# Second MLP product by Strassen's scheme on one core, with the second norm ahead of the MLP

## The chip, the cores and the metric

The kernel runs on one core of a Trainium2 chip. Its time is the device time of one execution in microseconds. A profiled execution has a time of its own and a span, from its first instruction to its last. The engines are called TensorE (PE in the rows; PEld is its weight load), VectorE (DVE), ScalarE (ACT), GpSimd (POOL) and SyncE (SP, here only a queue that issues DMAs).

## What is computed

One layer of a decoder over 512 tokens of width 1024, in float32. The attention part ends in the residual `x`; what matters here follows it:

```python
merged = gates[:, :, 0] * (y_a @ w_branch_a[l]) + gates[:, :, 1] * (y_b @ w_branch_b[l])
x = x + merged @ w_out[l]
h2 = rmsnorm(x, mlp_norm_g[l])
x = x + jnp.square(jax.nn.relu(h2 @ w_ff1[l])) @ w_ff2[l]
return rmsnorm(x, final_norm_g)
```

The hidden width is 4096: `w_ff1` is 1024 x 4096, `w_ff2` 4096 x 1024.

## The kernel before

All large products keep float32 accuracy with three matmuls in a rounded format (F32R): an operand is split into a rounded part `hi` and the rest `lo`, and `mm3` (lines 141 to 146) sums hi·hi, hi·lo and lo·hi in one PSUM buffer. Weights come by DMA as 128 x 1024 blocks into four raw buffers (`wr_p`, tag wraw); `pre` (lines 106 to 125) casts the block to `hi` on ScalarE (line 122) and subtracts to get `lo` on VectorE (line 124). `use` asks for a block and for the next two of a fixed list.

TensorE runs in the order of the code. For the other engines and the DMA queue a planner orders the instructions ahead of time, by when it expects them to be ready, the earlier in the code first; each engine then works through its list in order and waits where an operand or a buffer is not ready. PSUM has four buffers of 128 x 512 for the products (`pl_tile`).

The output projection (`out_proj`, lines 852 to 865) does, for each of four blocks of 128 tokens, two column halves of 24 matmuls; VectorE adds them to the residual `acc`, and the sum times the gain of the second norm goes to `xg` (line 863; GpSimd, for block 3 VectorE). `h2_block` (lines 867 to 875) transposes `xg` on TensorE, behind the first half of the next block, splits the result into `h2h` and `h2l`, and takes the sum of squares. The factor of the norm itself is not applied there: relu and square let its square, `r2`, be multiplied in behind the second product (line 918).

The MLP (lines 882 to 984) has 8 groups of 4 hidden blocks of 128. The first product of a hidden block is 24 matmuls of 512 tokens (`ff1_mm`); blocks 0 and 1 are done in halves of 256 tokens around `h2_block(3)` (lines 951 to 956). `ff1` takes relu (ScalarE), the square both on GpSimd and rounded on ScalarE, and their difference on VectorE. The second product of a group (`ff2`) is, for each of 4 token blocks and 2 column halves, 12 matmuls into one PSUM buffer and one VectorE instruction that scales and adds to `acc`. Between groups TensorE goes from the second product of one to the first product of the next; the last group's first product is done ahead of the second product before it, so the last two second products follow one another directly. In the last group `final` (lines 923 to 947) makes the final norm: squares on ScalarE, product with the gain and the root on GpSimd, scaling on ScalarE and VectorE, and the stores.

Of the kernel before, what the change touches and what calls it, by code (L numbers as in the profile page):

```python
# [21 lines left out]
NB = S // 128  # L22
# [27 lines left out]
def body(nc, tc, ctx, a, out, dbg=lambda name, ap: None):  # L50
# [10 lines left out]
    def sbpool(st, name, bufs=1, side="left"):  # L61
        return st.enter_context(tc.tile_pool(name=name, bufs=bufs, side=side, reuse_waits="tile"))
# [8 lines left out]
    def utile(i, dt, name):  # L71
        return u_p.tile([128, 4, S], dt, tag=f"u{i}", name=name)
# [11 lines left out]
    def pl_tile():  # L84
        return psL.tile([128, S], F32, tag="pl", name="pl")
# [15 lines left out]
        src["out", i] = a["wout"][i * 128:(i + 1) * 128]  # L101
    for i in range(32):
        src["ff1", i] = a["wff1"][i]
        src["ff2", i] = a["wff2"][i * 128:(i + 1) * 128]

    def pre(key):
        if key in W:
            return
        wh = pools.get(key[0], wh_p)
        if key[0] == "ff2":  # L110
            wh = wh2 if key[1] % 8 < 4 else ff["w"]
# [12 lines left out]
        eng.tensor_tensor(lo, raw, hi.bitcast(F32), op=ALU.subtract)  # L124
        W[key] = (hi, lo)
# [678 lines left out]
    pools["ff2"] = wh2  # L804
    mgh = m_p.tile([128, NK, S], F32R, name="mgh")
    mgl = m_p.tile([128, NK, S], F32R, name="mgl")
    gt = {}
# [68 lines left out]

    for b in range(NB):
        out_proj(b, b - 1 if b else None)
    dbg("x2", acc)


    FG = 4
    ff_st = ExitStack()
    ff = {}
    Z = {}

    def ff1_mm(p, f, lo=0, hi=S):
        wh_, wl_ = W["ff1", f]
        mm3(p[:, lo:hi], [(wh_[:, k], wl_[:, k], h2h[k][:, lo:hi], h2l[k][:, lo:hi]) for k in range(NK)])

    def ff1(f, p=None):
        use(("ff1", f), 2 if f < 30 else 31 - f)
        g, j = divmod(f, FG)
        if j == 0:
            Z[g] = (utile(2 * (g % 2), F32R, "zh"), utile(2 * (g % 2) + 1, F32R, "zl"))
        zh, zl = Z[g]
        if p is None:
            p = pl_tile()
            ff1_mm(p, f)
        r = ff["p"].tile([128, S], F32, tag="r", name="r", bufs=2)  # L900
        act.activation(r, p, AF.Relu)  # L901
        sq = ff["p"].tile([128, S], F32, tag="sq", name="sq", bufs=2)
        pool.tensor_tensor(sq, r, r, op=ALU.mult)  # L903
        act.activation(zh[:, j], r, AF.Square)
        dve.tensor_tensor(zl[:, j], sq, zh[:, j].bitcast(F32), op=ALU.subtract)  # L905

    def ff2(g):
        zh, zl = Z[g]
        w2 = [W["ff2", FG * g + j] for j in range(FG)]
        last = g == 32 // FG - 1  # L910
        for b in range(NB):
            sl = slice(b * 128, (b + 1) * 128)
            cuts = (0, 512, 768, 1024) if last and b == NB - 1 else (0, 512, 1024)
            for e, (lo, hi) in enumerate(zip(cuts, cuts[1:])):
                cs = slice(lo, hi)
                p = pl_tile()[:, :hi - lo]
                mm3(p, [(zh[:, j, sl], zl[:, j, sl], w2[j][0][:, cs], w2[j][1][:, cs]) for j in range(FG)])
                dve.scalar_tensor_tensor(acc[:, b, cs], p, r2[:, b:b + 1], acc[:, b, cs], op0=ALU.mult,  # L918
                                         op1=ALU.add)
                if last:  # L920
                    final(b, e, cs)
# [27 lines left out]
    ng = 32 // FG  # L949
    use(("ff1", 0))  # L950
    p01 = [pl_tile() for _ in range(2)]
    ff1_mm(p01[0], 0, 0, 256)
# [5 lines left out]
    ff["p"] = sbpool(ff_st, "ff", 2, "right")  # L958
    ff["w"] = sbpool(ff_st, "wh3", 4, "right")
    for j in range(FG):  # L960
        ff1(j, p01[j] if j < 2 else None)
        if j == 0:
            rsqrt_mean(r2, ss2, D)
            pool.tensor_tensor(r2, r2, r2, op=ALU.mult)
            xf = ff["p"].tile([128, 1, 512], F32, name="xf", bufs=1)
            fo = {}
            ss3 = cst.tile([128, 3 * NB], F32, name="ss3")
            r3 = cst.tile([128, NB], F32, name="r3")
        pre(("ff2", j))
    for g in range(ng):  # L970
        if g == 2:
            gf = ff["p"].tile([128, D], F32, name="gf", bufs=1)
            sp.dma_start(gf, bc(a["gfin"], [128, D]))
            pool.tensor_scalar(gf, gf, float(D) ** 0.5, None, op0=ALU.mult)
        early = FG if g == ng - 2 else 1
        if g + 1 < ng:
            for j in range(early):
                ff1(FG * (g + 1) + j)
            for j in range(FG):
                pre(("ff2", FG * (g + 1) + j))  # L980
# [51 lines left out]
```

## Time and profile before

| | |
|---|---|
| runs, median (lowest to highest) | 719.27 us (718.83 to 719.3) of 3 |
| profiled execution, time | 719.13 us |
| its span | 717.4 us |
| mean granted TensorE clock | 0.998 |
| busy: TensorE, VectorE, ScalarE, GpSimd | 705.0, 431.9, 305.8, 210.0 us |
| output projection ends, MLP begins | 360.87 us |

A row of a timeline gives the start in the span, the duration, engine, line, operation, what is written from what, the shape and the number of instructions merged; in brackets the idle time of the engine ahead of it and what ended that. Matmuls overlap: the distance of two starts is what one costs in a dense stretch.

### The profile page before, as it was taken

Reading aid. Unit: us, or ns where it says so; the run is one execution under the profiler, and the core shown is the slowest. Engines: PE = TensorE matmul, PEld = TensorE weight load, DVE = VectorE, ACT = ScalarE, POOL = GpSimd, SP = SyncE. Lnnn points to the kernel's source line nnn. Section 1 sums busy time; section 2 is a strip of 40 time slices with the busy share of each in tenths; the row PEclk is TensorE's granted clock in tenths of the full one; section 3 lists DMA queues with packets and bytes.
Section 4 is the critical chain, followed back from the end, with each engine's and each line's share of the span. In section 5 each row is a group of like instructions: output and inputs, shape, how many; then the busy total and the mean of one; then the engine's idle time right before and its main releaser. Section 6 shows DMA issues by size and latency. Waiting matters only on the chain.

```text
span 717.4 us, 10009 instructions
## 1 busy us (share of the span) xinstructions
PE 705.0 (98%) x3731; PEld 571.2 (80%) x3732; DVE 431.9 (60%) x804; ACT 305.8 (43%) x546; POOL 210.0 (29%) x236
## 2 busy tenths in 40 slices
PE   9999999999999999999999999999999999999996
PEld 7879787768765777888898888888888888888885
DVE  6487899999998855682357353353534535335233
ACT  6566777654643536651355051330513315035013
POOL 2315487663165531322132021020201203012012
PEclk9999999999999999999999999999999999999999
DMA  8632522113301128870056052241502415021002
GB/s 315 226 111 89 154 89 74 45 48 99 116 33 46 46 89 313 288 265 28 1 176 227 8 176 59 87 148 30 176 29 89 147 29 176 30 64 56 0 20 97
DMA packets 25953, 77.16 MB, mean 108 GB/s; under 512 B 3569, under 2 KB 4465, under 8 KB 25905
## 3 DMA queue, kind: packets, MB, share of 16 engines
q1 hardware_dynamic: 25040, 75.45, 31.5%
q10 hardware_dynamic: 864, 1.08, 0.4%
q8 instruction: 29, 0.48, 0.3%
q14 instruction: 20, 0.16, 0.1%
HBM read 69.31 MB, written 6.29 MB: 105 GB/s over the span
## 4 chain that ended last, share of the span: by engine, by line
PE 83%; DVE 12%; issue 1%; DMA 1%; POOL 1%; ACT 1%; SPq 0%; POOLq 0%; DVEq 0%; ACTq 0%
PE pl L144 19%; PE pl L145 19%; PE pl L146 19%; PE pl L240 3%; PE pl L241 3%; PE pl L242 3%; DVE nmx L593 2%; DVE oh L717 2%; PE pl L850 2%; PE pl L848 2%; PE pl L849 2%; DVE sc L404 2%; DVE m L403 2%; PE po L761 1%; PE pa L240 1%
## 5 line engine op out<-in xcount | busy, mean ns | idle before, releaser
L122 ACT ACTIVATE whi<-wraw 128x1024 fp32r<-128x1024 f32 (+1 forms) x103 | 108.0, 1053 | 217.4 <-PE pl L146 88.7
L124 DVE TENSOR_TENSOR wlo<-wraw,whi 128x1024 fp32r<-128x1024 f32 (+1 forms) x92 | 118.7, 1298 | 81.3 <-ACT whi L122 80.8
L903 POOL TENSOR_TENSOR sq<-r 128x512 f32<-128x512 f32 x32 | 49.2, 1540 | 245.7 <-ACT r L901 245.7
L144 PE MATMUL pl<-h2h,whi 128*128 128x512 f32 (+1 forms) x272 | 102.5, 377 | 0.0
L145 PE MATMUL pl<-h2l,whi 128*128 128x512 f32 (+1 forms) x272 | 102.4, 377 | 0.0
L146 PE MATMUL pl<-h2h,wlo 128*128 128x512 f32 (+1 forms) x272 | 102.4, 377 | 0.0
L146 PE MATMUL pl<-whi,zl 128*128 128x512 f32 (+1 forms) x260 | 100.3, 386 | 0.0
L145 PE MATMUL pl<-wlo,zh 128*128 128x512 f32 (+1 forms) x260 | 100.3, 386 | 0.0
L144 PE MATMUL pl<-whi,zh 128*128 128x512 f32 (+1 forms) x260 | 100.3, 386 | 0.0
L918 DVE SCALAR_TENSOR_TENSOR acc<-pl,r,acc 128x512 f32<-128x512 f32 (+1 forms) x65 | 48.2, 741 | 86.2 <-PE pl L146 86.2
L146 PEld LDWEIGHTS pl<-h2h,wlo 128*128 128x128 f32 x272 | 51.2, 188 | 9.4
L144 PEld LDWEIGHTS pl<-h2h,whi 128*128 128x128 f32 x272 | 51.2, 188 | 9.4
L145 PEld LDWEIGHTS pl<-h2l,whi 128*128 128x128 f32 x272 | 51.2, 188 | 9.3
L144 PEld LDWEIGHTS pl<-whi,zh 128*128 128x128 f32 x260 | 48.8, 188 | 9.9
L146 PEld LDWEIGHTS pl<-whi,zl 128*128 128x128 f32 x260 | 48.8, 188 | 9.9
L145 PEld LDWEIGHTS pl<-wlo,zh 128*128 128x128 f32 x260 | 48.8, 188 | 9.8
L717 DVE TENSOR_SCALAR oh<-posbc,thr 128x400 bf16<-128x400 f32 (+31 forms) x128 | 46.0, 411 | 3.9 <-PE pl L738 3.9
L598 POOL TENSOR_SCALAR pra<-pra,rs 128x400 f32<-128x400 f32 (+31 forms) x32 | 34.4, 1082 | 35.4 <-DVE rs L597 35.3
L240 PE MATMUL pl<-hh,whi 128*128 128x512 f32 x112 | 44.7, 399 | 0.0
L242 PE MATMUL pl<-hh,wlo 128*128 128x512 f32 x112 | 43.7, 390 | 0.0
L241 PE MATMUL pl<-hl,whi 128*128 128x512 f32 x112 | 43.7, 390 | 0.0
L905 DVE TENSOR_TENSOR zl<-sq,zh 128x512 fp32r<-128x512 f32 x32 | 22.8, 713 | 29.6 <-POOL sq L903 29.6
(287 smaller groups left out, 1305.7 us busy)
## 6 DMA issues: line engine op xcount, KB each, us to landing
wraw<-wff SPq DMA_DIRECT2D x64, 512.0 KB, 3.6
wraw<-wF SPq DMA_DIRECT2D x24, 512.0 KB, 3.3
gd<-gt SPq DMA_DIRECT2D x16, 256.0 KB, 2.2
wraw<-wbr SPq DMA_DIRECT2D x8, 512.0 KB, 4.2
wraw<-wout SPq DMA_DIRECT2D x8, 512.0 KB, 5.3
gx<-gd SPq DMA_DIRECT2D x16, 256.0 KB, 3.9
xtok<-x SPq DMA_DIRECT2D x4, 512.0 KB, 10.7
acc<-x SPq DMA_DIRECT2D x1, 2048.0 KB, 10.4
```

What stands on the lines that cost most here:

```text
L122: act.activation(hi, raw, AF.Copy)
L124: eng.tensor_tensor(lo, raw, hi.bitcast(F32), op=ALU.subtract)
L144: pe.matmul(ps, lh, rh, start=(i == 0), stop=False)
L145: pe.matmul(ps, lh, rl, start=False, stop=False)
L146: pe.matmul(ps, ll, rh, start=False, stop=(i == n - 1))
L240: pe.matmul(p, h[:, k], hh[k], start=(k == 0), stop=False)
L241: pe.matmul(p, h[:, k], hl[k], start=False, stop=False)
L242: pe.matmul(p, l[:, k], hh[k], start=False, stop=(k == NK - 1))
L598: pool.tensor_scalar(pr, pr, rs, None, op0=ALU.mult)
L717: dve.tensor_scalar(oh[:, :n], posbc[:, :n], thr[:, 4 * G + q:4 * G + q + 1], None, op0=ALU.is_le)
L903: pool.tensor_tensor(sq, r, r, op=ALU.mult)
L918: dve.scalar_tensor_tensor(acc[:, b, cs], p, r2[:, b:b + 1], acc[:, b, cs], op0=ALU.mult, op1=ALU.add)
```

## The change

The second norm is applied in front: behind each block of the output projection ScalarE squares `acc`, GpSimd takes the root, and VectorE multiplies by root and gain, before the block is transposed. Hidden blocks 0 to 2 instead of 0 and 1 are done in halves, all three first halves ahead of `h2_block(3)`, all second halves behind it.

The second product of a group (512 tokens x 512 hidden x 1024 columns) becomes one step of Strassen's scheme in Winograd's form. Z is cut into 2 x 2 blocks A of 256 tokens x 256 hidden, w_ff2 into blocks B of 256 hidden x 512 columns. Instead of eight block products there are seven, in the order of `ORDER`, on sums S of A's blocks (GpSimd, 512 elements a lane) and T of B's (GpSimd, 1024). Each operand is then split by `put_a` and `put_b` (cast on ScalarE, subtraction on VectorE). A `unit` is one product for 128 tokens: 6 matmuls of 512 columns into one PSUM buffer, and one or two VectorE adds into `acc` or into the sums U and V, which stay over all groups. In the last group `finish` combines them with `acc`. Raw blocks of B share the four raw buffers with w_ff1; there are six buffers of split B operands, three each of S and T.

```diff
-        src["ff2", i] = a["wff2"][i * 128:(i + 1) * 128]
...
-    wh2 = sbpool(right, "wh2", 4, "right")
     m_st = ExitStack()
+    wh2 = sbpool(m_st, "wh2", 4, "right")
...
             dve.tensor_tensor(acc[:, b, cs], p, acc[:, b, cs], op=ALU.add)
-            (dve if b == 3 else pool).tensor_tensor(xg[b][:, cs], acc[:, b, cs], g2bc[:, cs], op=ALU.mult)
             if e == 0 and prev is not None:
                 h2_block(prev)
+        act.activation(xg[b], acc[:, b], AF.Square, accum_out=ss2[:, b:b + 1])
+        rsqrt_mean(r2[:, b:b + 1], ss2[:, b:b + 1], D)
+        for e in range(2):
+            cs = slice(512 * e, 512 * e + 512)
+            dve.scalar_tensor_tensor(xg[b][:, cs], acc[:, b, cs], r2[:, b:b + 1], g2bc[:, cs], op0=ALU.mult,
+                                     op1=ALU.mult)
...
-        act.activation(xg[b], acc[:, b], AF.Square, accum_out=ss2[:, b:b + 1])
...
+    NG = 8
+    Z, AS, BS, RAW, TT, SS = {}, {}, {}, {}, {}, {}
+    ORDER = (("A11", "B11"), ("S2", "T2"), ("S1", "T1"), ("S4", "B22"), ("A12", "B21"), ("S3", "T3"),
+             ("A22", "T4"))
+    NP = len(ORDER)
+    NBS = 6
...
     def ff1(f, p=None):
-        use(("ff1", f), 2 if f < 30 else 31 - f)
-        g, j = divmod(f, FG)
...
+        g, i = divmod(f, 4)
+        j, q = divmod(i, 2)
         if p is None:
+            use(("ff1", f), min(2, 31 - f))
             p = pl_tile()
             ff1_mm(p, f)
-        r = ff["p"].tile([128, S], F32, tag="r", name="r", bufs=2)
-        act.activation(r, p, AF.Relu)
-        sq = ff["p"].tile([128, S], F32, tag="sq", name="sq", bufs=2)
-        pool.tensor_tensor(sq, r, r, op=ALU.mult)
-        act.activation(zh[:, j], r, AF.Square)
-        dve.tensor_tensor(zl[:, j], sq, zh[:, j].bitcast(F32), op=ALU.subtract)
+        if q == 0:
+            Z[g, j] = z_p.tile([128, 2, S], F32, tag=f"z{j}", name=f"z{j}", bufs=1)
+        z = Z[g, j][:, q]
+        act.activation(z, p, AF.Relu)
+        act.activation(z, z, AF.Square)
+
+    def raws(g):
+        for key in ("B11", "B12", "B22", "B21"):
+            j, n = int(key[1]) - 1, int(key[2]) - 1
+            r = wr_p.tile([128, 1024], F32, tag="wraw", name="wraw").rearrange("p (q d) -> p q d", q=2)
+            rows = slice((4 * g + 2 * j) * 128, (4 * g + 2 * j + 2) * 128)
+            sp.dma_start(r, a["wff2"][rows, 512 * n:512 * n + 512].rearrange("(q p) d -> p q d", p=128))
+            RAW[g, key] = r
+
+    def operand_a(g, key):
...
+            t = SS[g, key] = z_p.tile([128, 2, 256], F32, tag="s", name=key, bufs=3)
+            if key == "S1":
+                pool.tensor_tensor(t, z0[:, :, t1], z1[:, :, t1], op=ALU.add)
+            elif key == "S2":
+                pool.tensor_tensor(t, operand_a(g, "S1"), z0[:, :, t0], op=ALU.subtract)
+            elif key == "S3":
+                pool.tensor_tensor(t, z0[:, :, t0], z0[:, :, t1], op=ALU.subtract)
+            else:
+                pool.tensor_tensor(t, z1[:, :, t0], operand_a(g, "S2"), op=ALU.subtract)
+        return SS[g, key]
+
+    def operand_b(g, key):
...
+            t = TT[g, key] = wt_p.tile([128, 2, 512], F32, tag="t", name=key, bufs=3)
+            x, y = {"T1": ("B12", "B11"), "T2": ("B22", "T1"), "T3": ("B22", "B12"), "T4": ("B21", "T2")}[key]
+            pool.tensor_tensor(t, operand_b(g, x), operand_b(g, y), op=ALU.subtract)
+        return TT[g, key]
+
+    def put_a(g, k):
...
+        x = operand_a(g, ORDER[k][0])
+        act.activation(hi, x, AF.Copy)
+        dve.tensor_tensor(lo, x, hi.bitcast(F32), op=ALU.subtract)
+        AS[g, "op", k] = (hi, lo)
+
+    def put_b(g, k):
+        x = operand_b(g, ORDER[k][1])
+        t = bs_p.tile([128, 2, 2, 512], F32R, tag="b", name="b", bufs=NBS)
+        act.activation(t[:, 0], x, AF.Copy)
+        dve.tensor_tensor(t[:, 1], x, t[:, 0].bitcast(F32), op=ALU.subtract)
+        BS[g, k] = (t[:, 0], t[:, 1])
+
+    BLOCK = {0: (0, 0), 3: (0, 1), 4: (0, 0), 5: (1, 1), 6: (1, 0)}
+
+    def unit(g, k, m, cuts=(0, 512)):
+        p = pl_tile()
...
+            mm3(p[:, c], [(ah[:, q, ms], al[:, q, ms], bh[:, q, c], bl[:, q, c]) for q in range(2)])
+            i, n = BLOCK.get(k, (0, 0))
+            b = 2 * i + m
...
+            if k in BLOCK:
+                add(acc[:, b, cs])
+            if k == 0:
+                first(U[:, m])
+            elif k == 1:
+                add(U[:, m])
+            elif k == 2:
+                first(V[:, m])
+            if g == NG - 1:
+                finish(k, m, b, n, cs)
+
+    def finish(k, m, b, n, cs):
+        c12, c21, c22 = acc[:, m, 512:], acc[:, 2 + m, :512], acc[:, 2 + m, 512:]
+        if k == 1:
+            pool.tensor_tensor(c21, c21, U[:, m], op=ALU.add)
+        elif k == 2:
+            pool.tensor_tensor(V[:, m], U[:, m], V[:, m], op=ALU.add)
+            pool.tensor_tensor(c12, c12, V[:, m], op=ALU.add)
+        elif k == 5:
+            pool.tensor_tensor(c21, c21, c22, op=ALU.add)
+            dve.tensor_tensor(c22, c22, V[:, m], op=ALU.add)
+        if k >= 3:
+            final(b, n, cs)
+
+    def puts(g, k):
+        n = NP * g + k + NBS
+        if n < NP * NG:
+            put_b(*divmod(n, NP))
+        if g + 1 < NG and (k % 2 or k == NP - 1):
+            for kk in range(k - k % 2, min(k - k % 2 + 2, NP)):
+                put_a(g + 1, kk)
 
     def ff2(g):
...
+        if g + 1 < NG:
+            raws(g + 1)
+        if g < NG - 1:
+            for k in range(NP):
+                for m in range(2):
+                    unit(g, k, m)
+                puts(g, k)
+        else:
+            for k in range(NP - NBS):
+                for m in range(2):
+                    unit(g, k, m)
+                puts(g, k)
+            for m in range(2):
+                for k in range(NP - NBS, NP):
+                    unit(g, k, m, (0, 256, 512) if m and k == NP - 1 else (0, 512))
...
+    for j in range(3):
+        use(("ff1", j), 2 - j)
+        p0.append(pl_tile())
+        ff1_mm(p0[j], j, 0, 256)
     h2_block(3)
-    ff1_mm(p01[1], 1, 0, 256)
-    for j in range(2):
-        ff1_mm(p01[j], j, 256, S)
+    for j in range(3):
+        ff1_mm(p0[j], j, 256, S)
     m_st.close()
...
+    pool.tensor_tensor(acc[:, 2:4, :512], acc[:, 2:4, :512], acc[:, 2:4, 512:], op=ALU.subtract)
+    raws(0)
+    for j in range(4):
+        ff1(j, p0[j] if j < 3 else None)
+    for k in range(NP):
+        put_a(0, k)
+        if k < NBS:
+            put_b(0, k)
+    for g in range(NG):
+        if g + 1 < NG:
+            for j in range(4):
+                ff1(4 * (g + 1) + j)
...
         ff2(g)
```

`final` keeps its work with `e` counted in order of arrival of the column halves; its buffers move to places of the first norm's data.

## Rows read from the trace of the kernel before

**Rows 1.** Busy time, share of the span and instructions of each engine (page, part 1).

```profile
PE 705.0 (98%) x3731; PEld 571.2 (80%) x3732; DVE 431.9 (60%) x804; ACT 305.8 (43%) x546; POOL 210.0 (29%) x236
```

**Rows 2.** Busy time in one stretch of the MLP; columns in the first row.

```profile
core 0: us, PE busy (x) PEld busy (x) DVE busy (x) ACT busy (x) POOL busy (x), PEclk, DMA share, GB/s
...
400.00:450.00 50.00, 50.00 (x222) 41.41 (x221) 20.69 (x23) 12.73 (x16) 6.46 (x4) 1.00 0.27 85
```

**Rows 3.** The chain that ended last, shares by line (page, part 4).

```profile
PE pl L144 19%; PE pl L145 19%; PE pl L146 19%; PE pl L240 3%; PE pl L241 3%; PE pl L242 3%; DVE nmx L593 2%; DVE oh L717 2%; PE pl L850 2%; PE pl L848 2%; PE pl L849 2%; DVE sc L404 2%; DVE m L403 2%; PE po L761 1%; PE pa L240 1%
```

**Rows 4.** Timeline of TensorE in a first product: two starts three matmuls apart.

```profile
377.36 0.39 PE L144 MATMUL pl<-h2h,whi 128*128 128x512 f32 x1
...
378.04 0.39 PE L144 MATMUL pl<-h2h,whi 128*128 128x512 f32 x1
```

**Rows 5.** Timeline of TensorE around block 3: transposes, then half products of 256 columns.

```profile
363.75 1.04 PE L872 MATMUL pt<-ident,xg 128*128 128x128 f32 x8
364.54 0.36 PE L144 MATMUL pl<-h2h,whi 128*128 128x256 f32 x1
...
366.41 0.28 PE L144 MATMUL pl<-h2h,whi 128*128 128x256 f32 x1
...
366.77 0.28 PE L144 MATMUL pl<-h2h,whi 128*128 128x256 f32 x1
```

**Rows 6.** VectorE add, ScalarE copy and square around block 3 (timelines of both).

```profile
361.07 0.69 DVE L862 TENSOR_TENSOR acc<-pl,acc 128x512 f32<-128x512 f32 x1 [0.43 <-PE pl L850]
...
364.38 1.09 ACT L873 ACTIVATE h2h<-pt 128x512 fp32r<-128x512 f32 x2
365.35 1.06 ACT L875 ACTIVATE xg<-acc 128x1024 f32<-128x1024 f32 x1
```

**Rows 7.** The end of the kernel, timeline of all engines.

```profile
710.59 0.28 PE L146 MATMUL pl<-whi,zl 128*128 128x256 f32 x1
...
712.02 0.19 POOL L937 TENSOR_TENSOR r<-ss 128x1 f32<-128x1 f32 x1 [1.40 <-ACT o L928]
712.29 0.55 POOL L938 TENSOR_TENSOR r<-r,mhalf 128x1 f32<-128x1 f32 x1
712.87 0.91 ACT L942 ACTIVATE o<-xf,r 128x256 f32<-128x256 f32 x2 [0.93 <-POOL r L938]
```

**Rows 8.** Groups by line and shape from 240 us to the end: busy us, mean ns.

```profile
L122 ACT ACTIVATE whi<-wraw 128x1024 fp32r<-128x1024 f32 x76 | 79.8, 1057 | 204.8 <-PE pl L146 88.7 <-PE pl L145 63.1 <-DMA wraw<-wff 47.4
...
L918 DVE SCALAR_TENSOR_TENSOR acc<-pl,r,acc 128x512 f32<-128x512 f32 x63 | 47.2, 749 | 85.7 <-PE pl L146 85.7
...
L904 ACT ACTIVATE zh<-r 128x512 fp32r<-128x512 f32 x32 | 20.1, 629 | 0.7
```

**Rows 9.** DMA issues: source, count, KB each, us to landing (page, part 6).

```profile
wraw<-wff SPq DMA_DIRECT2D x64, 512.0 KB, 3.6
```

**Rows 10.** Timeline of VectorE: two instructions back to back, 512 and 1024 elements.

```profile
332.26 1.29 DVE L874 TENSOR_TENSOR h2l<-pt,h2h 128x512 fp32r<-128x512 f32 x2 [0.38 <-ACT h2h L873]
...
358.28 2.36 DVE L124 TENSOR_TENSOR wlo<-wraw,whi 128x1024 fp32r<-128x1024 f32 x2 [0.86 <-ACT whi L122]
```

**Rows 11.** GpSimd: two of 512 elements back to back; 1024 elements, ns min/median/max.

```profile
325.90 2.54 POOL L863 TENSOR_TENSOR xg<-acc,g2bc 128x512 f32<-128x512 f32 x2 [10.11 <-DVE acc L862]
...
L124 POOL TENSOR_TENSOR wlo<-wraw,whi x11: 2382/2402/3792, 83.3 to 180.2; 128x1024 fp32r<-128x1024 f32 x11
```

**Rows 12.** GpSimd and VectorE at the same moments (timelines of both).

```profile
301.11 2.13 POOL L827 TENSOR_TENSOR gx<-gx 128x512 f32<-128x512 f32 x1 [4.21 <-DVE gx L826]
...
300.89 1.21 DVE L124 TENSOR_TENSOR wo<-wraw,wo 128x1024 fp32r<-128x1024 f32 x1
...
375.18 1.51 DVE L905 TENSOR_TENSOR zl<-sq,zh 128x512 fp32r<-128x512 f32 x1 [1.71 <-POOL sq L903]
...
332.03 1.30 POOL L863 TENSOR_TENSOR xg<-acc,g2bc 128x512 f32<-128x512 f32 x1 [3.60 <-DVE acc L862]
...
374.11 2.04 POOL L903 TENSOR_TENSOR sq<-r 128x512 f32<-128x512 f32 x2
```

More of the change, by code (lines that the diff above doesn't have):

```diff
@@ L109, in pre @@
         wh = pools.get(key[0], wh_p)
-        if key[0] == "ff2":
-            wh = wh2 if key[1] % 8 < 4 else ff["w"]
         ap = src[key]
@@ L799, in body @@
     acc = acc_p.tile([128, NB, D], F32, name="acc")
-    wh2 = sbpool(right, "wh2", 4, "right")
     m_st = ExitStack()
+    wh2 = sbpool(m_st, "wh2", 4, "right")
     m_p = sbpool(m_st, "m", 1, "right")
     pools["out"] = wh2
-    pools["ff2"] = wh2
     mgh = m_p.tile([128, NK, S], F32R, name="mgh")
@@ L879, in body @@
     dbg("x2", acc)
-    FG = 4
+    NG = 8
     ff_st = ExitStack()
-    ff = {}
-    Z = {}
+    Z, AS, BS, RAW, TT, SS = {}, {}, {}, {}, {}, {}
[3 more added lines that the diff above has]
+    NBS = 6
     def ff1_mm(p, f, lo=0, hi=S):
@@ L902, in ff1 @@
-        sq = ff["p"].tile([128, S], F32, tag="sq", name="sq", bufs=2)
-        pool.tensor_tensor(sq, r, r, op=ALU.mult)
-        act.activation(zh[:, j], r, AF.Square)
-        dve.tensor_tensor(zl[:, j], sq, zh[:, j].bitcast(F32), op=ALU.subtract)
-    def ff2(g):
[L908 to L921, printed above, removed]
@@ L923, in final @@
-    def final(b, e, cs):
-        if e == 0:
-            fo[b] = ff["p"].tile([128, D], F32, tag="o", name="o", bufs=2)
+        if q == 0:
[10 more added lines that the diff above has]
+            RAW[g, key] = r
@@ new lines, in operand_a @@
+    def operand_a(g, key):
+        z0, z1 = Z[g, 0], Z[g, 1]
+        t0, t1 = slice(0, 256), slice(256, 512)
+        if key[0] == "A":
+            return (z0, z1)[int(key[2]) - 1][:, :, (t0, t1)[int(key[1]) - 1]]
+        if (g, key) not in SS:
+            t = SS[g, key] = z_p.tile([128, 2, 256], F32, tag="s", name=key, bufs=3)
[8 more added lines that the diff above has]
+        return SS[g, key]
@@ new lines, in operand_b @@
+    def operand_b(g, key):
+        if key[0] == "B":
+            return RAW[g, key]
+        if (g, key) not in TT:
+            t = TT[g, key] = wt_p.tile([128, 2, 512], F32, tag="t", name=key, bufs=3)
[3 more added lines that the diff above has]
+    def put_a(g, k):
+        if k % 2 == 0:
+            AS[g, k // 2] = utile(k // 2, F32R, "as")
+        t = AS[g, k // 2]
+        hi, lo = (t[:, 2 * (k % 2) + i].rearrange("p (q t) -> p q t", q=2) for i in range(2))
+        x = operand_a(g, ORDER[k][0])
+        act.activation(hi, x, AF.Copy)
+        dve.tensor_tensor(lo, x, hi.bitcast(F32), op=ALU.subtract)
+        AS[g, "op", k] = (hi, lo)
@@ new lines, in put_b, with add, first @@
+    def put_b(g, k):
[7 more added lines that the diff above has]
+        p = pl_tile()
+        ah, al = AS[g, "op", k]
+        bh, bl = BS[g, k]
+        ms = slice(m * 128, (m + 1) * 128)
+        for lo, hi in zip(cuts, cuts[1:]):
+            c = slice(lo, hi)
+            mm3(p[:, c], [(ah[:, q, ms], al[:, q, ms], bh[:, q, c], bl[:, q, c]) for q in range(2)])
+            i, n = BLOCK.get(k, (0, 0))
+            b = 2 * i + m
+            cs = slice(512 * n + lo, 512 * n + hi)
+            def add(t):
+                dve.tensor_tensor(t, p[:, c], t, op=ALU.add)
+            def first(t):
+                if g == 0:
+                    act.activation(t, p, AF.Copy)
+                else:
+                    add(t)
+            if k in BLOCK:
[8 more added lines that the diff above has]
+                finish(k, m, b, n, cs)
@@ new lines, in puts @@
+    def puts(g, k):
[5 more added lines that the diff above has]
+                put_a(g + 1, kk)
+    def ff2(g):
+        if g + 1 < NG:
[5 more added lines that the diff above has]
+                puts(g, k)
+        else:
+            for k in range(NP - NBS):
[5 more added lines that the diff above has]
+                    unit(g, k, m, (0, 256, 512) if m and k == NP - 1 else (0, 512))
@@ L926, in final @@
+    parts = {b: 0 for b in range(NB)}
+    def final(b, n, cs):
+        e = parts[b]
+        parts[b] += 1
         o = fo[b]
@@ L929, in final @@
         if e == 0:
-            pool.tensor_tensor(xf[:, 0], acc[:, b, cs], gf[:, cs], op=ALU.mult)
+            pool.tensor_tensor(xf[b], acc[:, b, cs], gf[:, cs], op=ALU.mult)
             dve.tensor_scalar(s3[:, 0:1], s3[:, 0:1], D * EPS, None, op0=ALU.add)
-        if cs.stop < D:
+            first0[b] = cs.start
+        if e == 0 or cs.stop % 512:
             if e:
@@ L940, in final @@
         step = 256 if b == NB - 1 else 512
+        f0 = first0[b]
         for lo in range(0, 512, step):
-            act.activation(o[:, lo:lo + step], xf[:, 0, lo:lo + step], AF.Copy, scale=r)
-            act.dma_start(out[rows, lo:lo + step], o[:, lo:lo + step])
-        for lo in range(512, 1024, step):
+            q = slice(f0 + lo, f0 + lo + step)
+            act.activation(o[:, q], xf[b][:, lo:lo + step], AF.Copy, scale=r)
+            act.dma_start(out[rows, q], o[:, q])
+        for lo in range(512 - f0, 1024 - f0, step):
             q = slice(lo, lo + step)
@@ L947, in final @@
             sp.dma_start(out[rows, q], o[:, q])
[L949 to L952, printed above, removed]
+    p0 = []
+    for j in range(3):
+        use(("ff1", j), 2 - j)
+        p0.append(pl_tile())
+        ff1_mm(p0[j], j, 0, 256)
     h2_block(3)
-    ff1_mm(p01[1], 1, 0, 256)
-    for j in range(2):
-        ff1_mm(p01[j], j, 256, S)
+    for j in range(3):
+        ff1_mm(p0[j], j, 256, S)
     m_st.close()
-    ff["p"] = sbpool(ff_st, "ff", 2, "right")
@@ L959, in body @@
[L959 to L972, printed above, removed]
+    z_p = sbpool(ff_st, "z", 1, "right")
@@ new lines, in body @@
+    wt_p = sbpool(ff_st, "wt", 1, "right")
+    bs_p = sbpool(ff_st, "bs", 1, "right")
+    ss3 = cst.tile([128, 3 * NB], F32, name="ss3")
+    r3 = cst.tile([128, NB], F32, name="r3")
+    first0 = {}
+    U = z_p.tile([128, 2, 512], F32, name="U")
+    V = z_p.tile([128, 2, 512], F32, name="V")
+    pool.tensor_tensor(acc[:, 2:4, :512], acc[:, 2:4, :512], acc[:, 2:4, 512:], op=ALU.subtract)
[6 more added lines that the diff above has]
+            put_b(0, k)
@@ L973, in body @@
+    for g in range(NG):
+        if g + 1 < NG:
+            for j in range(4):
+                ff1(4 * (g + 1) + j)
+        if g == NG - 2:
+            uo = [utile(4 + i, F32, f"o{i}") for i in range(4)]
+            fo = [uo[b // 2][:, 2 * (b % 2):2 * (b % 2) + 2].rearrange("p a b -> p (a b)") for b in range(NB)]
+            gf = uo[2][:, 0:2].rearrange("p a b -> p (a b)")
+            xf = [uo[2][:, 2], uo[2][:, 3], uo[3][:, 0], uo[3][:, 1]]
             sp.dma_start(gf, bc(a["gfin"], [128, D]))
@@ L974, in body @@
             pool.tensor_scalar(gf, gf, float(D) ** 0.5, None, op0=ALU.mult)
[L975 to L980, printed above, removed]
         ff2(g)
-        if g + 1 < ng:
-            for j in range(early, FG):
-                ff1(FG * (g + 1) + j)
     ff_st.close()
```

3 lines of the change are left out of this document (removed).

## The prediction, made before the change was run

> **What bounds the kernel now.** I read the busy shares first: TensorE is busy 98% of the span, VectorE 60%, ScalarE 43%, GpSimd 29% [rows 1]. A busy TensorE need not be one at its peak, so next came the stretches of the MLP: in 50 us of it TensorE is never idle, its granted clock is 1.00, and the DMA engines have a share of 0.27 [rows 2]. The chain that ended last then says which line carries the end: the three matmuls of the helper that sums hi·hi, hi·lo and lo·hi, 19% of the span each [rows 3]. So from the end of the output projection to the last matmul the time is a count of matmuls times their step. The step is the distance of two starts, not the duration that a row shows: three 512-column matmuls begin every 0.68 us [rows 4], 0.227 each; three 256-column ones every 0.36, 0.120 each [rows 5]. All other engines work under this cover, and the question is what of their new work looks out from under it.
>
> **The sum is made against the profiled execution:** 719.13 us, a span of 717.4 and 1.7 around it; the median of the runs shown, 719.27, lies 0.14 above.
>
> **Matmuls.** The second product was 8 groups x 4 token blocks x 2 column halves x 12 matmuls = 768; it becomes 8 groups x 7 products x 2 blocks x 6 = 672. 96 x 0.227 = 21.8 us less. A third hidden block is now done in halves: 24 x (0.240 - 0.227) = 0.3 more. Net **-21.5**.
>
> **Norm in front.** For blocks 0 to 2 the transposes now wait for add 0.69, square 1.06 [rows 6], 1.15 with the read of its sum, the two GpSimd steps of the root 0.85 (712.02 to 712.87) [rows 7] and two multiplies, 0.75 each at most [rows 8]; with hand-offs of 0.05 some 4.4 us. Their cover is the next block's 24 matmuls, 5.4 us: 0, and if the cover failed, the excess three times. Block 3 has three half products ahead of it, 72 x 0.120 = 8.6 us: 0. But behind its transposes came a half product that did not need them; now the next matmul does. Transposes end at 364.54 [rows 5]; copy (0.55) and subtraction (0.69) let the second matmul start near 365.7 [rows 6]: **+1.0**, bounds 0.5 and 1.5. The squares on GpSimd, the root behind the MLP and the scale in the adds disappear from engines with idle time: 0.
>
> **First loads.** Four raw blocks of w_ff2 are fetched ahead of hidden block 3's weights, through the same four raw buffers. The first is given back only after a difference on GpSimd and a split into buffers that lie where the output projection's operands lay, at the earliest behind block 3's transposes (8.6 + 0.8 = 9.4 us after the projection). Split 1.05, load 3.6 [rows 9], split 1.05 + 1.22: 16.4; TensorE wants the block at 9.4 + 1.0 + 8.6 = 19.0. GpSimd has a 2.4 us subtraction on acc and up to three differences of 2.4 in the way. Bounds 0 and 4.6; I take **+1.0**, near the row sum that says hidden.
>
> **A full group on the other engines.** TensorE: 96 + 84 matmuls = 40.8 us, 21.8 of it first product, 19.0 second. VectorE instructions issued back to back follow at 0.61 us for 512 elements and 1.14 for 1024 [rows 10]: 16 adds out of PSUM 9.8, 7 splits of B 8.0, 7 splits of A 4.3, 4 splits of w_ff1 4.6: 26.7. GpSimd: 1.24 for 512, 2.4 for 1024 [rows 11]: four sums of A and four of B, 14.6. ScalarE: 11 casts of 1024 and 15 instructions of 512, at 1.06 and 0.63 [rows 8]: 21. DMA: eight loads of 512 KB, as many as before, 0.27 share: 0.
>
> No engine reaches 40.8, but the second product is dense. There VectorE has 9.8 + 8.0 + 4.3 = 22.1 us for 19.0 of matmuls, and its first add waits for the first unit (6 matmuls, 1.4): it falls 22.1 + 1.4 - 19.0 = 4.5 us behind. A unit needs the PSUM buffer of the fourth before it, so TensorE tolerates three units, 4.1 us. What is left is 0.4, taken as 0.5; seven groups **+3.5**. The queue is the point: a split ahead of an add on VectorE delays the PSUM buffer, though the split itself is not due for five products. In the first product behind it VectorE has 17 us free and catches up.
>
> A rule against this step: the Trainium skill, Advanced Engine Details and Errata, The Read-Write Bubble, says that on VectorE the memory latency is exposed between instructions. By it each instruction would cost its whole 0.69 or 1.22, the stretch 24.4 us, the arrears 6.8 and the stall 2.7 a group, and the sum 16 us higher. The paired rows (2 in 1.29, 2 in 2.36) [rows 10] speak against it, so the sum keeps 0.61 and 1.14.
>
> What GpSimd adds to these arrears the trace shows only in kind. A GpSimd op on two SBUF inputs took 2.13 us instead of 1.3 when a VectorE subtraction of two SBUF inputs had begun before it, and such a subtraction took 1.51 instead of 0.69 when GpSimd was first [rows 12]: one waits for the end of the other. A VectorE op with one input in PSUM ran beside a 1.30 us GpSimd op at full speed [rows 10, 12]; the 16 adds are of this kind. Lower bound 0 (the B sums depend on loads alone and can run under the first product), upper bound all 14.6 a group. I take 0, near the free rows, since 17 us of the first product are open; the other end is a rival.
>
> **The last group.** Each half of the tokens sends through GpSimd four combining adds, two products with the gain (1.24 each) and two roots (0.85): 9.1, for both 18.3 us. The first is due after the third unit, when TensorE has 11 units, 15.0 us, to go. So GpSimd ends 18.3 + 0.7 - 15.0 = 4.0 us behind TensorE, where today it ends 2.0 behind (710.87 to 712.84) [rows 7]: +2.0. No first product stands ahead of this group, so it inherits VectorE's arrears, 4.0: together **+6.0**. Bounds: 2.0 without arrears; 12 if GpSimd also waits for VectorE's two-SBUF ops there (some 6 us).
>
> **Sum:** -21.5 + 1.0 + 1.0 + 3.5 + 6.0 = -10.0. 719.13 - 10.0 = 709.1, against the median **709.3 us**. A measurement of this kernel can tell about 0.2%, 1.4 us, from no change.
>
> **Rivals.**
> - **Clean** (0.13): the splits stand behind the adds in VectorE's queue, no stalls, no arrears: -21.5 + 1.0 + 2.0 = 700.8. For it: the splits are due late. Against: they are ready early.
> - **A long end** (0.15): the upper bound of the last group and half of that of the loads: 709.3 + 6.0 + 1.3 = 716.6. For it: GpSimd's 18.3 us form nearly one chain with VectorE between.
> - **GpSimd holds VectorE up in every second product; slower** (0.16). Place: VectorE's queue between two adds. Three of four A sums need the whole hidden group, so they run in the dense stretch; if two B differences do too and each catches a waiting split on average half through, 2 x 1.2 = 2.4 us a group go on top of the stall: 709.3 + 7 x 2.4 = 726.1. It decides from (717.8 - 709.3)/7 = 1.2 us a group (no gain left) and from 1.6 (slower). For it: [rows 12]. Against: free time in the first product. The Trainium skill, Perfetto Trace Analysis, Optimizing Scalar/DVE Operations, warns that moving work between these two might not help, as they share a port; this rival is that warning at work.
> - **Every instruction at its full shown duration** (0.04): 709.3 + 16 = 725, for which [rows 10] speak least. It is the rule named above.
>
> **How the numbers follow.** Forecast 0.52, clean 0.13, long end 0.15 (a quarter of it within 0.2%), held up 0.16 (0.01 within), full duration 0.04 (half within). Faster by over 0.2%: 0.52 + 0.13 + 0.11 = 0.76; within: 0.04 + 0.01 + 0.02 = 0.07; slower: 0.15 + 0.02 = 0.17. The forecast's own range, from stalls of 0 to 0.9 a group and an end of 2 to 8, is 702 to 714. For 8 in 10 the range reaches up over the long end and the first part of the held-up case: 702 to 722.
>
> **What would show it.** Right: about 672 matmuls on the second product; TensorE gaps of about half a us late in each second product, released by VectorE adds; none in the out projection, one of 1 us behind block 3's transposes; the last matmul ending near 695 and 12.5 us from there to the span's end (6.5 today), GpSimd nearly without pause in them. Wrong: gaps of 2 us and more a group ahead of units, VectorE splits of 1.9 us and longer beside GpSimd differences (held up); no gaps and an end of 8.5 or less (clean); a matmul step other than 0.227, or a granted clock under 1.00, would refute the base of the sum.

## The result: slower, and the profile after

The changed kernel takes **748.41 us** (747.92 to 750.48), the kernel before beside it 719.28: a ratio of **1.041**, interval 1.039 to 1.043. The forecast was 709.3 us. Busy shares, clock, and the chain that ended last, on the page of the profile after:

```profile
PE 696.4 (93%) x3653; PEld 559.2 (75%) x3654; DVE 555.1 (74%) x920; ACT 364.0 (49%) x630; POOL 301.2 (40%) x276
...
PEclk9999999999999999999999999999999999999996
...
PE 25%; DVE 14%; issue 4%; POOL 3%; ACT 2%; DMA 1%; POOLq 0%; DVEq 0%
PE pl L141 9%; PE pl L143 8%; PE pl L142 8%; DVE b L961 5%; DVE as L954 4%; DVE acc L979 2%; DMA wraw<-wff 1%; ACT b L960 1%; DVE V L979 1%; POOL T L944 1%; DVE U L979 0%; POOL acc L1004 0%; POOL V L1003 0%; DVE wlo L121 0%; DVE acc L1007 0%
```

TensorE was busy 98% of a span of 717.4 [rows 1] and is busy 93% of 746.7; its work shrank (705.0 to 696.4 us), the time grew. The chain used to be TensorE's three matmul lines at 19% each [rows 3]; they now hold 8 to 9% each, and VectorE's splits (`b` L961, `as` L954) have come in. The waits of TensorE say for what (total, times, longest):

```profile
PE pl L141 <- DVE acc L979: 26.5, 8, 8.0
PE pl L141 <- DVE V L979: 7.3, 7, 2.5
PE pl L143 <- DVE wlo L121: 2.9, 1, 2.9
```

In the MLP of the kernel before there is no gap between two matmul starts [rows 2, 4]. Now there are 40.6 us of gaps (distances of starts beyond the step). Three lines of stretches (length, then busy time of PE, PEld, DVE, ACT, POOL, granted clock, DMA share, GB/s) show what follows some of them:

```profile
384.40:387.00 2.60, 2.60 (x8) 2.08 (x9) 2.60 (x3) 2.07 (x4) 0.00 (x0) 0.65 1.00 296
387.00:390.00 3.00, 3.00 (x12) 2.36 (x11) 1.35 (x2) 0.00 (x0) 0.00 (x0) 0.74 0.96 348
...
432.40:436.00 3.60, 3.55 (x9) 2.80 (x10) 3.60 (x5) 0.00 (x0) 0.00 (x0) 0.58 0.21 36
```

Behind gaps of 3.06 us (up to 384.40) and 3.24 us (up to 432.45) the granted clock drops to its lower level: starts 0.425 us apart instead of 0.227, for 3.4 us. This happens four times, at 1.4 to 1.6 us each. A fifth time it falls inside the gap of 8 us at the end, where only six half matmuls follow, some 0.6 us in all.

A steady group's second product begins at 594.4. First the two places where TensorE stops, then VectorE and GpSimd around them:

```profile
606.20 0.50 PE L141 MATMUL pl<-b,as 128*128 128x512 f32 x1 [0.76 <-DVE V L979]
614.52 0.47 PE L141 MATMUL pl<-b,as 128*128 128x512 f32 x1 [2.57 <-DVE acc L979]
```

```profile
601.13 3.21 DVE L961 TENSOR_TENSOR b<-wraw,b 128x1024 fp32r<-128x1024 f32 x1 [0.20 <-ACT b L960]
...
605.46 1.28 DVE L979 TENSOR_TENSOR V<-pl,V 128x512 f32<-128x512 f32 x2
...
610.31 3.46 DVE L954 TENSOR_TENSOR as<-S,as 128x512 fp32r<-128x512 f32 x2
613.69 1.27 DVE L979 TENSOR_TENSOR acc<-pl,acc 128x512 f32<-128x512 f32 x2
```

```profile
600.86 2.39 POOL L944 TENSOR_TENSOR T<-wraw 128x1024 f32<-128x1024 f32 x1
605.68 1.29 POOL L933 TENSOR_TENSOR S<-z 128x512 f32<-128x512 f32 x1 [2.43 <-DVE as L954]
610.47 2.76 POOL L944 TENSOR_TENSOR T<-wraw,T 128x1024 f32<-128x1024 f32 x1 [3.49 <-DVE b L961]
```

A split of B that takes 1.22 alone takes 3.21 beside the difference of 600.86; two splits of A that take 1.29 take 3.46 beside the one of 610.47. Each is some 2 us, and behind each stand two product adds (605.46, 613.69) that give PSUM buffers back. TensorE runs out of them twice a group: the two starts come 0.91 and 2.72 us later than the step, in five groups nearly to the digit; the first group loses 3.24 us, the seventh 5.37. The add at 605.46 itself runs beside GpSimd at full speed: it reads PSUM.

### The profile page after: what moved, and what is told of

Read it like the earlier page. It is cut to its first block, busy times and chain, and to the rows that moved or that the text cites. A ratio compares the mean times of both kernels' runs of the same rounds, so it can differ in the third digit from the quotient of the medians.

```text
span 746.7 us, 10090 instructions
## 1 busy us (share of the span) xinstructions
PE 696.4 (93%) x3653; PEld 559.2 (75%) x3654; DVE 555.1 (74%) x920; ACT 364.0 (49%) x630; POOL 301.2 (40%) x276
## 5 line engine op out<-in xcount | busy, mean ns | idle before, releaser
L121 DVE TENSOR_TENSOR wlo<-wraw,whi 128x1024 fp32r<-128x1024 f32 (+1 forms) x60 | 86.0, 1437 | 56.8 <-ACT whi L119 56.1
L141 PE MATMUL pl<-b,as 128*128 128x512 f32 (+1 forms) x226 | 91.2, 404 | 34.2 <-DVE acc L979 26.5
L119 ACT ACTIVATE whi<-wraw 128x1024 fp32r<-128x1024 f32 (+1 forms) x71 | 74.7, 1052 | 98.4 <-PE pl L142 61.3
L141 PE MATMUL pl<-h2h,whi 128*128 128x512 f32 (+1 forms) x280 | 104.9, 375 | 0.3 <-ACT h2h L874 0.3
L143 PE MATMUL pl<-b,as 128*128 128x512 f32 (+1 forms) x226 | 90.0, 398 | 0.0
L142 PE MATMUL pl<-b,as 128*128 128x512 f32 (+1 forms) x226 | 89.5, 396 | 0.0
L944 POOL TENSOR_TENSOR T<-wraw 128x1024 f32<-128x1024 f32 x16 | 42.2, 2634 | 101.2 <-DMA wraw<-wff 101.2
L979 DVE TENSOR_TENSOR acc<-pl,acc 128x512 f32<-128x512 f32 (+1 forms) x81 | 52.4, 674 | 40.0 <-PE pl L143 37.0
L141 PEld LDWEIGHTS pl<-b,as 128*128 128x128 f32 x226 | 43.7, 193 | 49.2 <-ACT as L953 17.8
L143 PEld LDWEIGHTS pl<-h2h,wlo 128*128 128x128 f32 x280 | 53.1, 190 | 12.5 <-DVE wlo L121 3.3
L944 POOL TENSOR_TENSOR T<-wraw,T 128x1024 f32<-128x1024 f32 x16 | 42.5, 2654 | 42.1 <-DVE b L961 24.0
L960 ACT ACTIVATE b<-T 128x1024 fp32r<-128x1024 f32 x32 | 33.7, 1057 | 45.2 <-PE pl L143 44.9
L143 PEld LDWEIGHTS pl<-b,as 128*128 128x128 f32 x226 | 43.6, 193 | 9.2
L142 PEld LDWEIGHTS pl<-b,as 128*128 128x128 f32 x226 | 43.8, 194 | 8.7
L961 DVE TENSOR_TENSOR b<-wraw,b 128x1024 fp32r<-128x1024 f32 x24 | 43.2, 1802 | 1.4 <-ACT b L960 1.2
```

The lines of the kernel that those rows point to most:

```text
L141: pe.matmul(ps, lh, rh, start=(i == 0), stop=False)
L142: pe.matmul(ps, lh, rl, start=False, stop=False)
L143: pe.matmul(ps, ll, rh, start=False, stop=(i == n - 1))
L944: pool.tensor_tensor(t, operand_b(g, x), operand_b(g, y), op=ALU.subtract)
L960: act.activation(t[:, 0], x, AF.Copy)
L961: dve.tensor_tensor(t[:, 1], x, t[:, 0].bitcast(F32), op=ALU.subtract)
```

## The experiments

**Leave the differences out, or move them.** The first run splits a raw block in place of each T; every T subtraction is left out.

```diff
+        return RAW[g, {"T1": "B12", "T2": "B22", "T3": "B12", "T4": "B21"}[key]]
```

> Left out: the four differences T of w_ff2's blocks on GpSimd (a raw block is split in the place of each), so the second product is not the reference's. Theory H (GpSimd's differences hold VectorE's queue up in the dense second product): in the changed kernel a split of B took 3.21 us for 1.22 and a pair of A splits 3.46 for 1.28, 4.2 us a group; without them the 3.6 us of TensorE gaps in each of seven groups go: 748.4 - 25 = 723, give or take 3. Theory Q (VectorE's own load and the order of its queue, splits ahead of adds, make the gaps and the lock is incidental): the gaps stay, 745 to 749.

712.75 us (one execution): no gap in the first six groups, 40.8 us from one to the next, the forecast's ideal, and 1.2 us of gaps in the seventh. It is 10 us under H's number because the price had other places too: the wait for `wlo` is gone (2.9 us), and so are the four drops of the clock (6.0 us). What is left in the seventh group has the same form: there GpSimd scales the gain of the final norm (653.41, 2.78 us) and sums A behind it, and two VectorE splits beside that take 2.08 for 1.22 and 1.78 for 0.68 us (656.44 and 660.77). The second run computes T, on VectorE:

```diff
-            pool.tensor_tensor(t, operand_b(g, x), operand_b(g, y), op=ALU.subtract)
+            dve.tensor_tensor(t, operand_b(g, x), operand_b(g, y), op=ALU.subtract)
```

> The four differences T run on VectorE instead of GpSimd. Theory H: the two that fall into the dense stretch cost VectorE 1.14 us each in place of 4.2 us of waiting: 1.9 us a group less, 748 - 13 = 735, give or take 4. Theory Q: VectorE has 4.6 us more a group, 2.3 of it in the dense stretch, so each group's gap grows by about that: 748 + 16 = 764.

719.42 us (one execution), below both numbers. VectorE gets 32 instructions of 1.22 us more, and still the gaps of the seven groups go from 26.8 to 1.7 us (0.5 in the first, 1.2 in the seventh). So VectorE was not short of time; it was held. H's number took it that TensorE gets back only what VectorE saves, which this run does not bear out. The last group's gaps grow, from 9.75 to 13.8 us. Does the amount of GpSimd's work count, or its place? The third run moves two of four:

```diff
-            pool.tensor_tensor(t, operand_b(g, x), operand_b(g, y), op=ALU.subtract)
+            (dve if key in ("T3", "T4") else pool).tensor_tensor(t, operand_b(g, x), operand_b(g, y), op=ALU.subtract)
```

> The changed kernel (748.4 us) with two of the four differences of a group's raw blocks, T3 and T4, on VectorE and T1 and T2 left on GpSimd. Theory H (a difference on GpSimd costs time only where it holds up a split that has product adds behind it in VectorE's queue: T3 and T4 run in the second product, T1 and T2 in the first one, where VectorE has nothing urgent): nearly all of the time comes back, 722 us, 719 to 725. Rival Q (GpSimd's work costs by its amount, wherever it runs): half of the 29 us between this kernel and the one with all four on VectorE (719.4) comes back, 734 us, 731 to 737.

718.81 us (ratio 0.9995, interval 0.9985 to 1.0005): moving half the differences gives back all of it, not half. (The other half, T1 and T2 alone on VectorE, was not run.) The waits of TensorE in the first six groups, in the changed kernel (405 to 683 us) and then in this one (405 to 653; total, times, longest):

```profile
PE pl L141 <- DVE acc L979: 15.9, 6, 3.1
PE pl L141 <- DVE V L979: 3.8, 5, 0.8
```

```profile
PE pl L141 <- DVE acc L979: 0.3, 1, 0.3
```

The groups of VectorE in the MLP (busy us, mean ns), first the changed kernel, then this one:

```profile
L961 DVE TENSOR_TENSOR b<-wraw,b 128x1024 fp32r<-128x1024 f32 x24 | 43.2, 1802 | 1.4 <-ACT b L960 1.2
L954 DVE TENSOR_TENSOR as<-S,as 128x512 fp32r<-128x512 f32 x32 | 40.6, 1292 | 0.1
```

```profile
L961 DVE TENSOR_TENSOR b<-wraw,b 128x1024 fp32r<-128x1024 f32 x24 | 29.1, 1215 | 1.0 <-ACT b L960 1.0
...
L954 DVE TENSOR_TENSOR as<-S,as 128x512 fp32r<-128x512 f32 x32 | 23.3, 751 | 0.1
```

The same splits lose 31 us of apparent work, all of it waiting. GpSimd still holds VectorE up in this kernel, but where nothing is urgent, in the first product; GpSimd's row, then VectorE's:

```profile
608.46 2.39 POOL L944 TENSOR_TENSOR T<-wraw,T 128x1024 f32<-128x1024 f32 x1
```

```profile
608.64 3.30 DVE L121 TENSOR_TENSOR wlo<-wraw,whi 128x1024 fp32r<-128x1024 f32 x1 [4.22 <-ACT whi L119]
614.57 0.69 DVE L979 TENSOR_TENSOR acc<-pl,acc 128x512 f32<-128x512 f32 x1 [2.63 <-PE pl L143]
```

The split is 2.1 us late, and the next add comes 2.6 us after it.

**More PSUM.** The products go round eight PSUM buffers instead of four (`pa`, `po` and two `pt` buffers, idle by then):

```diff
-        p = pl_tile()
+        p = mm_tile()
```

> The MLP's units and hidden blocks rotate over eight PSUM buffers instead of four, so that an add may be seven units (9.5 us) late instead of three (4.1). If VectorE's arrears are bounded within a group (they are made up in the first product, as both theories H and Q say): no gaps in the seven groups, 748.4 - 25 = 723. If VectorE is short over whole groups, the gaps are only put off: above 735.

721.78 us (1.0042, 1.0026 to 1.0059), GpSimd's differences untouched. No gap in the seven groups. So in the groups TensorE stops for late buffers and nothing else, and the arrears do not grow from group to group. What is left over the ideal are the wait ahead of `wlo` (2.9 us) and 16.0 us in the last group, 11.6 of it one wait at the end.

**The same amount of GpSimd in the kernel before.** Behind each product add of the first seven groups GpSimd subtracts a piece of `acc` from itself into an unused buffer:

```diff
+                else:
+                    pool.tensor_tensor(xf[:, 0], acc[:, b, cs], acc[:, b, cs], op=ALU.subtract)
```

> The kernel before with, in each of its first seven second products, eight subtractions of 128x512 on GpSimd, one behind each product add, results unused: some 10 us of GpSimd in a group, as much as the four differences take alone. Theory H (GpSimd holds up only VectorE instructions with both operands in SBUF; the adds read PSUM, few splits run there, and each product of 12 matmuls leaves VectorE twice the time): no change, 718.9 to 720 us. Rival Q (GpSimd's work beside a dense second product costs VectorE or TensorE time by its amount): 7 times some 3.6 us, 740 us or more.

719.24 us (1.0003, 0.9994 to 1.0012). GpSimd, then VectorE, in one of these second products:

```profile
575.38 1.04 POOL L923 TENSOR_TENSOR xf<-acc 128x512 f32<-128x512 f32 x1 [1.68 <-DVE acc L918]
578.10 1.04 POOL L923 TENSOR_TENSOR xf<-acc 128x512 f32<-128x512 f32 x1 [1.68 <-DVE acc L918]
```

```profile
577.20 0.75 DVE L918 SCALAR_TENSOR_TENSOR acc<-pl,r,acc 128x512 f32<-128x512 f32 x1 [1.97 <-PE pl L146]
579.92 0.75 DVE L918 SCALAR_TENSOR_TENSOR acc<-pl,r,acc 128x512 f32<-128x512 f32 x1 [1.97 <-PE pl L146]
```

The instructions took 1.04 us, not 1.24, so 8.3 us a group. VectorE waits for TensorE 1.97 us ahead of each add, and hardly a split stands between: GpSimd's work by its amount alone costs nothing here. (By their starts these instructions follow the adds rather than meet them, so the run tests the stretch, not an add held directly.)

**The norm alone.** The kernel before, with the norm in front and hidden blocks 0 to 2 in halves:

> The kernel before with the norm in front alone (and hidden blocks 0 to 2 in halves, no Strassen scheme). My step of the prediction: +1.0 us, 720.3. Rival (the norm's chain holds TensorE at each block): 3 us or more, 722 and above. If the squares taken away from GpSimd and VectorE matter: below 719.

722.6 us (1.0049, 1.0034 to 1.0064): +3.5. That is the rival's number, but not its place: in the output projection TensorE never waits (first line, columns as above). Then come TensorE behind block 3's transposes, ScalarE at the same moment, and the stretch that follows:

```profile
314.00:360.00 46.00, 46.00 (x217) 38.37 (x216) 23.00 (x30) 11.91 (x18) 3.46 (x7) 1.00 0.20 60
```

```profile
370.99 0.38 PE L144 MATMUL pl<-h2h,whi 128*128 128x256 f32 x1 [1.19 <-ACT h2h L878]
372.37 0.39 PE L145 MATMUL pl<-h2l,whi 128*128 128x256 f32 x1 [0.99 <-DVE h2l L879]
```

```profile
369.40 1.06 ACT L122 ACTIVATE whi<-wraw 128x1024 fp32r<-128x1024 f32 x1 [6.18 <-PE pt L877]
370.36 1.07 ACT L878 ACTIVATE h2h<-pt 128x512 fp32r<-128x512 f32 x2
```

```profile
373.50:377.00 3.50, 3.50 (x19) 3.50 (x19) 0.00 (x0) 0.31 (x1) 2.78 (x1) 0.53 0.35 123
```

The cast of a weight block stands ahead of the copy that TensorE waits for (and its split, at 370.49 on VectorE, ahead of the subtraction); behind the wait the clock is at its lower level for 3.4 us. The run beside it puts the third half behind the transposes, as cover:

```diff
     for j in range(3):
+        if j == 2:
+            h2_block(3)
         ff1_mm(p01[j], j, 0, 256)
-    h2_block(3)
```

> The kernel before with the norm in front and three first halves, as in the run that cost 3.5 us, but with the third half placed behind block 3's transposes and not ahead of them. Theory H2 (the norm itself costs its 0.7 us at the start of the MLP; the rest was the wait behind the transposes with the lower clock that followed it): 719.8 us, 719.2 to 720.6. Rival (the norm in front of the MLP costs 3.5 us wherever the halves stand): 722 to 723 us.

719.4 us (1.0004, 0.9995 to 1.0014): no gap, no lower clock. The norm is free within the noise; the order of the halves cost 3.2 of the 3.5.

**The head of the changed kernel.** The same cover there, and hidden block 3's weights fetched ahead of the raw blocks (`pre(("ff1", 3))` before `raws(0)`):

> The changed kernel with hidden block 2's first half behind block 3's transposes again, and hidden block 3's weights fetched ahead of the first raw blocks of w_ff2. The trace shows 1.0 us of gaps behind the transposes, 3.1 us ahead of hidden block 3, and behind that a stretch at half the granted clock (384 to 389) that costs some 1.7: 5.8 together. If all are the head's own: 748.4 - 5.8 = 742.6. If the later group's gaps take it back: 746 and above.

747.07 us (1.0402, 1.038 to 1.042): 1.3 of the 6 us, and by their intervals the two ratios cannot be told apart. By the traces the gaps behind the transposes, 1.0 us, are gone; the wait for `wlo` is still 2.8 us, with the drop of the clock behind it. GpSimd, then VectorE:

```profile
378.16 3.23 POOL L944 TENSOR_TENSOR T<-wraw,T 128x1024 f32<-128x1024 f32 x1 [2.35 <-DVE b L961]
```

```profile
379.08 3.38 DVE L121 TENSOR_TENSOR wlo<-wraw,whi 128x1024 fp32r<-128x1024 f32 x1
```

The load was not late; the split was held by a difference, as in the groups. With all T on VectorE this gap is 0.7 us.

**The last group.** Its gaps are 0.46, 1.23 and 8.06 us, the longest ahead of the last half unit, which shares a PSUM buffer with the half before. Two runs: a buffer of its own for each half (`p = pl_tile()` moved into the loop over `cuts`), and the last group's second product as plain block products, U and V joined a group earlier.

> The changed kernel with a PSUM buffer of its own for each half of the last unit (they share one, and the second half waits 8.0 us for the first one's add). Theory C (the chain of combining adds on GpSimd and VectorE sets the end, and the second half's add waits for it anyway): the 8 us gap goes, but the last add moves only from 740.3 to about 738.6: 1.7 us, 746.7. Rival (the shared buffer sets the end): 8 us less, 740.

748.33 us (1.0400, 1.0375 to 1.0425). The gap shrinks to 3.09 and the last matmul starts at 735.8 instead of 739.8, but from its end to the span's end it is 9.9 us instead of 6.5: nothing gained. The rival is excluded; C's own gain of 1.7 us does not show either.

```diff
-            if g == NG - 1:
-                finish(k, m, b, n, cs)
+            if g == NG - 2:
+                finish(k, m)
```

> The changed kernel with the last group's second product plain (eight block products, 12 matmuls more), so that U and V are combined with acc a group earlier, beside matmuls. From the start of group 6's second product to the last matmul took 56.1 us. Theory C: it becomes 180 x 0.227 = 40.8, plus 0.2 for the halves and group 6's gaps of about 4 to 5: 45.5, and the whole 748.4 - 10.5 = 738. Rival (the last group is long because VectorE enters it in arrears, not because of the combining): those stay, and 2.7 us come on top: 746 to 751.

740.67 us (1.0294, 1.0277 to 1.0312), -7.7. From the start of the seventh second product to the last matmul it is 45.9 us instead of 56.0, as C said (45.5): what sets the end is the chain of joining adds on GpSimd and VectorE. The gaps there go from 15.1 to 4.6 us and 2.3 us of lower clock and slower steps go; twelve more matmuls and twelve more done in halves cost 2.8. The gaps of the groups before are as they were; some 2.4 us come back elsewhere, where the clock is low for longer in this execution (6.8 us instead of 3.4 in the first hidden blocks, two drops instead of one from the second group to the sixth).

**All three cures together:** T on VectorE, the plain last group, the cover in the head.

> Differences T on VectorE, last group plain, and the head as in e7_head, together. Theories H and C and the head's terms: no gaps from the output projection to the last matmul: 361.5 + 684 matmuls of the second product and 768 of the first, 331.2 us in all, + 6.5 to the span's end + 1.7 = 701, give or take 3. If VectorE, with T on it, still holds the end back: 706 to 712.

**706.35 us** (0.9825, 0.981 to 0.984). This misses the 701, give or take 3, and lies in the range given for its rival. But the rows do not show VectorE short of time: gaps of 4.9 us are left, nearly all where U and V are joined, and there VectorE waits for GpSimd:

```profile
666.66 0.69 DVE L980 TENSOR_TENSOR acc<-pl,acc 128x512 f32<-128x512 f32 x1 [1.18 <-POOL acc L1005]
669.26 0.69 DVE L980 TENSOR_TENSOR acc<-pl,acc 128x512 f32<-128x512 f32 x1 [1.91 <-POOL acc L1005]
```

So the joining adds go to VectorE as well (`pool` to `dve` in `finish`):

> The fastest variant so far (706.35 us) with the additions that join U, V and the quadrants one group before the end on VectorE and not on GpSimd: ten additions of 128x512. Theory C2 (the gaps of 4.9 us that are left stand there because the adds of later products wait for GpSimd's additions): 702 us, 701 to 703.5. Rival (VectorE is the one short of time there, and ten more of its instructions at 0.68 us replace the wait): 705.5 to 708 us.

**703.85 us** (0.979, 0.9775 to 0.9804), the best of all. It is 0.35 us above the range of C2, with gaps of 1.9 and 0.8 us left at the joins and 0.7 in the first group; the rival is excluded.

## Why the prediction was wrong, by its steps

- **GpSimd in a full group, "I take 0": the step that failed.** The gaps of the seven groups are 3.24 + 5 x 3.63 + 5.37 = 26.8 us (1.2 to 1.7 of them stay where the differences are gone or moved), and three drops of the clock behind them 4.5. I argued that the differences depend on loads alone and so fit in 17 free us of the first product. That holds for T1 and T2 (584.09 and 591.32 in the group shown). T3 and T4 depend on the queue and the buffers too: T3 follows directly on three sums of A, which need the whole hidden group (600.86), and T4 waits 3.49 us for a split of B (610.47). Both are for the next group, so nobody needs them there; in the run with both on VectorE they are computed in the next first product (at 635.21 and 639.21, where the second product ended at 632.0), and nobody misses them. The rival "GpSimd holds VectorE up" had place and mechanism right, two differences a group; its price was low, half an instruction each (2.4 a group) where they cost 2.0 and 2.2 of VectorE and 3.6 of TensorE, and it left out the head, the clock and the end, so its 726.1 is far off too. Its weight of 0.16 came from the same wrong reason. The rule named there, in the Trainium skill, Perfetto Trace Analysis, Optimizing Scalar/DVE Operations, agrees with these runs: the same four differences make the kernel 29 us slower on GpSimd than on VectorE.
- **Arrears of VectorE, +3.5: too much.** With two or four more instructions of 1.22 us a group VectorE let TensorE stop in none of the five middle groups, for 0.4 to 0.5 us in the first and 1.2 to 1.3 in the seventh. In the run with T3 and T4 on it, VectorE is busy for 17.2 of the second product's 19.0 us and its last add ends at 635.2, 3.2 us behind TensorE: the arrears are there, not 4.5 but 3.2, and under the 4.1 that TensorE tolerates. Instructions back to back cost 0.60 and 1.13 there (two adds from 634.01 to 635.21, a split from 617.14 to 618.27). The rule that the forecast weighed against its step, in the Trainium skill, Advanced Engine Details and Errata, The Read-Write Bubble, was read there as the whole duration for each instruction, and so read no run here bears it out: by these steps 2 x 0.60 - 1.13 = 0.07 us of an instruction does not grow with its size, an estimate.
- **First loads, +1.0: wrong size, wrong reason.** 2.9 us and 1.6 of lower clock. The load was in time (cast at 378.69); the split of hidden block 3's weights began only at 383.13, behind two splits of raw blocks that took 4.55 us for 2.36 beside a difference (378.66).
- **Norm, +1.0:** here right: the two waits behind the transposes are 0.5 us each. By itself the same order costs 3.5, since the cast ahead of the copy and the drop of the clock were not in the sum.
- **Last group, +6.0: right that it has a chain, wrong where it shows.** Not 12.5 us behind TensorE: that stretch is 6.5, as before. TensorE itself waits 9.75 us inside the group, and some 0.6 go to the lower clock behind the last wait.
- **Matmuls, -21.5: right.** In dense stretches starts stay 0.227 apart, and without the waits the change is worth 15.2 us (719.06 to 703.85), there with a plain last group, so with twelve matmuls more. That the clock would stay at 1.00 was part of this base and failed four times ahead of the end, 6.0 us.

Beyond the forecast: 31.3 - 3.5 in the groups, 4.5 - 1.0 at the first loads, 10.4 - 6.0 in the last group, and 0.7 by which the MLP of this execution began later (361.61 for 360.87; runs with the same code up to there begin at 360.89 to 361.55): 36 of 39 us. The rest lies in steps a tenth of a us longer around the gaps. Three slips in the prediction's sums move nothing: the way of the first loads adds up to 16.3, not 16.4; with all four GpSimd instructions in its way its upper bound is 7.0, not 4.6; seven stalls of 2.7 instead of 0.5 add 15.4, not 16.

## What to carry to other kernels

Before giving GpSimd work on SBUF operands, find when its own queue lets it start, and which VectorE instructions with both operands in SBUF run then: each cost VectorE here up to nearly its whole length (2.2 us of 2.4), and the PSUM adds queued behind were late by as much. Shorter products between PSUM evictions (here 6 matmuls for 12) halve the time that four buffers can bridge: three products, 4.1 us for 8.2. And a wait of TensorE may cost half as much again through the clock (2.9 and 1.6 us at the first loads).

## What the runs showed of the hardware that was not expected

- In the changed kernel's MLP, ten splits `as<-S` (both operands in SBUF) that began beside a running GpSimd instruction took 2.64 us on average, the other 22 took 0.68; fifty product adds (one operand in PSUM) that began beside one took 0.67 to 0.69 without exception. It holds the other way too: a difference of 2.39 took 3.39 and 3.25 when VectorE was first.
- The granted clock fell to its lower level, 1.2 GHz by the step of 0.425, behind gaps of TensorE of 2.4 us (the norm alone, two waits one matmul apart) to 3.4 us, but not behind each: in the changed kernel it followed the gap of the first group and the 2.7 us gaps of the fourth and the seventh, not those of the other four, and other ones in other runs. What tells them apart stays open.
